# Layer norms of a two-layer decoder trunk: the last column block of the second 128 rows in two half banks, and the modulation after it in program order

## The chip, the cores and the metric

The kernel runs on one core of one Trainium2 chip. The metric is the device time of one execution in microseconds (us). TensorE (PE) multiplies, VectorE (DVE) and ScalarE (ACT) do the elementwise work, GpSimd (POOL) a few tiny operations, and SyncE (SP) issues the loads of the weights. PE writes its products into eight PSUM banks of 512 float32 columns by 128 partitions.

## What is computed

The input is one sequence of 256 rows by 2048 columns in float32. There are two layers, and each has a token mixer (forgetting attention in layer 0, sliding-window attention in layer 1) and a gated feed-forward block. Around each of these four sub-layers stands the same frame:

```python
for i in range(DEPTH):
    h = x * (1.0 + sc1) + sh1
    y = fox_attention(h, ...) if i % 2 == 0 else swa_attention(h, ...)
    x = layer_norm(DEEPNORM_ALPHA * x + (1.0 + g1) * y, ln_mix_g[i], ln_mix_b[i])
    h = x * (1.0 + sc2) + sh2
    y = conv_ffn(h, ...)
    x = layer_norm(DEEPNORM_ALPHA * x + (1.0 + g2) * y, ln_ffn_g[i], ln_ffn_b[i])
```

A layer norm needs the mean and the variance of a whole row of 2048 columns. So the first multiplication of the next sub-layer can't start before the last column of the sub-layer before it is there. There are four such places: three between sub-layers (called the first, second and third boundary here), and the end of the program.

## The kernel before

All products are formed in float32 with a split of both operands: a value is the sum of a rounded high part and a low part, and each product is three matmuls (high by high, high by low, low by high). A weight tile `w` of 256 rows by 512 columns is loaded by SP, ACT rounds it into `wh` (L264), and DVE forms the low part `wl` (L275). `wh` and `wl` have four buffers each, used in turn, so the cast into a buffer waits until PE is through with the tile four places earlier. `stream` (L256) issues all this and keeps a few tiles ahead.

The rows lie in two halves of 128, `t` = 0 and 1. The products that end a sub-layer (the output projection of a mixer in `out_proj`, the down projection in `conv_ffn`) are formed in column blocks of 512 by `x_mm` (L285): for each of the two row halves one bank "xs", three matmuls of 512 columns for each of the K slices. In the last block `x_mm_end` (L294) changes the order: for the last `n` weight tiles (2 in the mixers, 2 and 4 in the two down projections) it does the first row half as the tiles come, keeps the tiles, and does the second row half at the end. So the first half can be evacuated while PE does the second.

`residual` (L620) evacuates a block on DVE, row half by row half: bank times gate (L623), add to `x` (L625), row statistics of these 512 columns (L630). In the last block follow the sums over all blocks (L633), adding epsilon (L635), and the power of minus one half on POOL (L636). For the first row half `nm`, minus mean times reciprocal deviation, is formed too (L629).

`between` (L1103) then leads to the next sub-layer. `normalise` (L640) scales a block of 512 columns in place, the first row half on ACT (L646), the second on DVE (L648). `mod_turn` (L485) transposes a pair of 128-column slices of `x` on PE into banks "sm" (L493), four transposes a pair. `mod_pair` (L497) applies scale and shift and splits the result into `hHL` (high part `hH`, low part `hL`). For the first two pairs it takes the short way: ACT writes `hH` out of the bank (L503), DVE the full value (L504) and `hL` (L505). The later pairs go by L507 on ACT, L508 on DVE, L84 on ACT (which needs both) and L85 on DVE. `modulate` (L515) runs two pairs at once and hangs the other six into a list `feeds`; each following weight tile calls one after its own matmuls. `feed` calls `normalise` for a block of 512 columns whenever its first slice is due.

After the first and third boundary comes the up projection: `u_mm` goes through a weight tile in eight pairs of matmuls, 512 columns of `hHL` (high and low part together) and 256 of `hH`. The tile number n, counted from 1, needs the slices of the pair number n. After the second boundary comes `x_stationary` with `hHL` as the stationary operand.

The order on each engine is made by a scheduler when the program is built, out of the order in which the code records the instructions. `pin` keeps an instruction in the recorded order against others that are pinned; others may be moved. At run time each engine works its list in that fixed order, so an instruction that waits holds up all behind it on its engine.

At the very end the last layer norm is applied on DVE with its weights (L1152, L1153) block by block, and SP issues the eight stores.

## Time and profile before

| | |
|---|---|
| median of three runs | 2256.86 us (2254.90, 2256.86, 2256.91) |
| the profiled execution: its time | 2256.56 us |
| its span on the core | 2254.8 us |
| mean granted TensorE clock | 0.988 |
| instructions | 33096 |
| DVE busy | 1847.4 us |
| ACT busy | 1220.7 us |
| bytes moved | 602.66 MB, 267 GB/s in the mean |

The views used below print one line for an instruction or for a group of them. A line of the timeline has the start and the length in us, the engine, the line of the kernel, the operation, output and input by name, shape and count; in brackets stands how long the engine sat idle before it, and who released it. A line of the windows view has the stretch and its length, then for each engine the time busy and the count, then the granted clock of TensorE (1.00 is full speed), the share of the DMA engines and GB/s. A line of the groups has the total busy time, the mean in ns, and the idle time before. TensorE matmuls are pipelined: the cadence is the distance of two starts, and the printed length of one is longer than that.

### The profile page before, as it was taken

How to read it: one execution, taken by the hardware profiler on the slowest of the kernel's cores; microseconds unless marked ns; L12 is line 12 of the kernel's file. 1: busy time of each engine (PE TensorE's matmuls, PEld its weight loads, DVE VectorE, ACT ScalarE, POOL GpSimd, SP SyncE). 2: the span in 40 equal slices, each digit the busy share in tenths (PEclk: the TensorE clock that was granted, in tenths of full speed). 3: DMA queues.
4: the chain of work that ended last, by engine and by line, in shares of the span. 5: the costliest groups of instructions: out<-in, count | busy, mean ns of one | idle time of the engine just before them, and what ended most of it. 6: DMA issues, size and time to landing. Idle time of an engine off the chain costs nothing. (4 is left out here: it accounts for less than half of the span.)

```text
span 2254.8 us, 33096 instructions
## 1 busy us (share of the span) xinstructions
PE 2196.5 (97%) x12037; PEld 1901.8 (84%) x12037; DVE 1847.4 (82%) x2626; ACT 1220.7 (54%) x2073; POOL 22.6 (1%) x52
## 2 busy tenths in 40 slices
PE   6999999999999999999999999999999999999997
PEld 5999888878888888888887788778888888888886
DVE  6979999979989968799888999769988655676766
ACT  3435656555555543655634588746555533555542
POOL 0000000000000000000000000000000000000000
PEclk9999999999999999999999999999999999999999
DMA  9999999958978989789887777648887555555553
GB/s 336 385 357 345 356 354 325 332 190 302 322 266 296 323 299 336 263 288 317 275 311 283 243 244 244 219 163 263 287 270 257 190 192 195 189 193 188 188 195 112
DMA packets 274228, 602.66 MB, mean 267 GB/s; under 512 B 21062, under 2 KB 29960, under 8 KB 273552
## 3 DMA queue, kind: packets, MB, share of 16 engines
q1 hardware_dynamic: 273008, 595.85, 76.5%
q0 software_dynamic: 1056, 4.69, 0.6%
q8 instruction: 94, 1.54, 0.3%
q14 instruction: 70, 0.57, 0.1%
HBM read 598.37 MB, written 2.10 MB: 266 GB/s over the span
## 5 line engine op out<-in xcount | busy, mean ns | idle before, releaser
L264 ACT CAST wh<-w 128x1024 fp32r<-128x1024 f32 x728 | 763.9, 1051 | 802.5 <-PE us L75 288.4
L275 DVE TENSOR_TENSOR wl<-w,wh 128x1024 fp32r<-128x1024 f32 x728 | 885.9, 1221 | 300.4 <-ACT wh L264 293.7
L75 PE MATMUL us<-hHL,wh 128*128 128x512 f32 x2816 | 985.7, 393 | 3.2 <-DVE hHL L505 3.2
L75 PE MATMUL us<-hHL,wl 128*128 128x256 f32 x2816 | 792.0, 283 | 3.2 <-DVE wl L275 3.2
L75 PEld LDWEIGHTS us<-hHL,wh 128*128 128x128 f32 x2816 | 530.2, 188 | 115.8 <-ACT hHL L503 3.9
L75 PEld LDWEIGHTS us<-hHL,wl 128*128 128x128 f32 x2816 | 534.4, 190 | 8.0 <-DVE wl L275 4.6
L75 PE MATMUL xs<-wh,gT 128*128 128x512 f32 x1408 | 435.7, 390 | 0.0
L75 PEld LDWEIGHTS xs<-wh,gT 128*128 128x128 f32 x1408 | 264.3, 188 | 54.8
L75 PE MATMUL xs<-wl,gT 128*128 128x512 f32 x704 | 273.9, 389 | 0.0
L75 PE MATMUL xs<-wh,hHL 128*128 128x512 f32 x704 | 238.5, 404 | 0.3 <-ACT wh L264 0.2
L404 DVE SCALAR_TENSOR_TENSOR acc<-wa,cact,acc 128x1024 f32<-128x1024 f32 x180 | 228.2, 1276 | 0.0
L75 PE MATMUL ws<-hHL,wh 128*128 128x256 f32 x1024 | 190.1, 288 | 4.4 <-ACT hHL L84 2.1
L75 PEld LDWEIGHTS ws<-hHL,wh 128*128 128x128 f32 x1024 | 162.0, 195 | 7.4 <-ACT hHL L84 2.7
L404 DVE SCALAR_TENSOR_TENSOR acc<-wa,cactp,acc 128x1024 f32<-128x1024 f32 x128 | 162.2, 1277 | 0.0
L75 PEld LDWEIGHTS xs<-wh,hHL 128*128 128x128 f32 x704 | 131.8, 190 | 30.0 <-issue 1.0
L75 PEld LDWEIGHTS xs<-wl,gT 128*128 128x128 f32 x704 | 132.2, 188 | 27.3
L75 PE MATMUL ws<-hHL,wl 128*128 128x256 f32 x512 | 143.7, 288 | 2.2 <-DVE wl L275 2.2
L75 PE MATMUL xs<-wl,hHL 128*128 128x512 f32 x352 | 141.7, 403 | 1.5 <-DVE wl L275 1.4
L75 PE MATMUL xs<-wh,oT 128*128 128x512 f32 x384 | 124.9, 395 | 0.1
L1069 ACT ACTIVATE u<-us,ccol 128x256 f32<-128x256 f32 x176 | 98.1, 562 | 39.4 <-DVE us L1067 39.4
L75 PEld LDWEIGHTS ws<-hHL,wl 128*128 128x128 f32 x512 | 98.4, 195 | 2.9 <-DVE wl L275 2.8
L1070 DVE SCALAR_TENSOR_TENSOR u<-us,ccol,u 128x255 f32<-128x255 f32 x176 | 83.3, 478 | 13.4 <-ACT u L1069 13.3
(217 smaller groups left out, 1753.3 us busy)
## 6 DMA issues: line engine op xcount, KB each, us to landing
w<-in_ffn_w_up_dram SPq DMA_DIRECT2D x352, 512.0 KB, 4.6
wa<-in_ada_w_dram SPq DMA_DIRECT2D x320, 512.0 KB, 5.4
w<-in_ffn_w_down_dram SPq DMA_DIRECT2D x176, 512.0 KB, 3.9
w<-in_fox_w_in_dram SPq DMA_DIRECT2D x96, 512.0 KB, 7.0
wo<-in_ada_w_dram SPq DMA_DIRECT2D x48, 512.0 KB, 9.3
w<-in_swa_w_in_dram SPq DMA_DIRECT2D x40, 512.0 KB, 5.6
w<-in_fox_w_o_dram SPq DMA_DIRECT2D x32, 512.0 KB, 5.5
w<-in_swa_w_o_dram SPq DMA_DIRECT2D x32, 512.0 KB, 5.3
```

The costliest lines, as they stand in the source:

```text
L75: return nc.tensor.matmul(o, lhsT, rhs, start=start, stop=stop, **kw)
L264: pin(nc.scalar.copy(h, w), False)
L275: pin(nc.vector.tensor_tensor(l, w, f32(h), op=ALU.subtract), behind[0] > 0)
L404: pin(nc.vector.scalar_tensor_tensor(ac, wo, (cactp if row else cact)[:, k:k + 1], ac, op0=ALU.mult, op1=ALU.add), True)
L1069: nc.scalar.activation(u, pf, AF.Identity, bias=cw(CW, f), scale=cw(2, f))
L1070: nc.vector.scalar_tensor_tensor(u[:, 1:], pf[:, :S - 1], cw(1, f), u[:, 1:], op0=ALU.mult, op1=ALU.add)
```

## The change

The last block's second row half goes into two banks ("xh") of which 256 columns each are used, instead of one bank of 512. In `x_mm`, each matmul of 512 columns into it becomes two of 256. In `x_mm_end` the kept tiles are gone through once for the first bank and then once for the second. The number of kept tiles goes from 2 to 3 in the mixers and in the first down projection, and stays at 4 in the second. `residual` evacuates each half bank with its own three instructions, and the row statistics of the second row half are taken over 256 columns everywhere (twelve sets: four of 512 columns for the first half, eight of 256 for the second). `nm` stands behind the first half bank.

In `modulate`, blocks 0 and 1 are normalised ahead of the first pair, block 2 with the pair at slice 4, and block 3 with the pair at slice 8. The two instructions of `normalise` and those of the first two pairs on DVE are now pinned. The larger `stats` is paid for in memory: three small tiles of the rotary angles move into one buffer of the temporary pool "t".

```diff
-    def x_banks():
-        return [bank("xs") for _ in range(NT)]
+    def x_banks(halved=False):
+        return [bank("xs") for _ in range(NT - 1)] + [[bank("xh")[:, :256] for _ in range(2)] if halved else bank("xs")]
...
+    def pieces(o):
+        return [(p, slice(n * 256, n * 256 + 256)) for n, p in enumerate(o)] if isinstance(o, list) else [(o, slice(0, WB))]
+
-    def x_mm(ps, kc, h, l, stat, last, first=0, ts=range(NT)):
+    def x_mm(ps, kc, h, l, stat, last, first=0, ts=range(NT), part=slice(0, 2)):
...
-                mm(ps[t], xh, h[:, i, :], start=kc + i == first)
-                mm(ps[t], xh, l[:, i, :])
-                mm(ps[t], xl, h[:, i, :], stop=kc + i == last)
+                for o, c in pieces(ps[t])[part]:
+                    mm(o, xh, h[:, i, c], start=kc + i == first)
+                    mm(o, xh, l[:, i, c])
+                    mm(o, xl, h[:, i, c], stop=kc + i == last)
...
-                for e in kept:
-                    x_mm(ps, *e, stat, nk - 1, ts=(1,))
+                for p in range(len(pieces(ps[1]))):
+                    for e in kept:
+                        x_mm(ps, *e, stat, nk - 1, ts=(1,), part=slice(p, p + 1))
...
-                nc.vector.tensor_scalar(o, ps[j], g, b, op0=ALU.mult, op1=ALU.add)
-                nc.vector.tensor_tensor(hL[:, k + j, :], o, f32(hH[:, k + j, :]), op=ALU.subtract)
+                pin(nc.vector.tensor_scalar(o, ps[j], g, b, op0=ALU.mult, op1=ALU.add), fixed)
+                pin(nc.vector.tensor_tensor(hL[:, k + j, :], o, f32(hH[:, k + j, :]), op=ALU.subtract), fixed)
...
-            if k % 4 == 0:
-                norm(k // 4)
-            mod_pair(G, B, k, mod_turn(k, 2), k < 4)
+            for d in {0: (0, 1), 4: (2,), 8: (3,)}.get(k, ()):
+                norm(d)
+            mod_pair(G, B, k, mod_turn(k, 2), k < 4, False, k < 4)
...
-    stats = cst.tile([P, NT, D // 512, nc.vector.BN_STATS_DIM], F32, name="stats")
+    stats = cst.tile([P, D // 512 + D // 256, nc.vector.BN_STATS_DIM], F32, name="stats")
...
+            for n, (o, c) in enumerate(pieces(ps[t])):
+                cx = slice(d * 512 + c.start, d * 512 + c.stop)
+                xs = x[:, t, cx]
+                nc.vector.tensor_tensor(tmp[:, c], o, gate[:, cx], op=ALU.mult)
+                nc.vector.tensor_tensor(xs, xs, tmp[:, c], op=ALU.add)
+                if last and t == 0:
+                    nc.vector.bn_stats(stats[:, d, :], xs)
+                elif last:
+                    for q in range(cx.start // 256, cx.stop // 256):
+                        nc.vector.bn_stats(stats[:, 4 + q, :], x[:, t, q * 256:(q + 1) * 256])
+                if last and t == 1 and end and n == 0:
+                    mu, rs, nm = moments[0]
+                    pin(nc.vector.scalar_tensor_tensor(nm, mu, -1.0, rs, op0=ALU.mult, op1=ALU.mult))
...
-                nc.scalar.activation(xs, xs, AF.Identity, scale=rs, bias=nm)
+                pin(nc.scalar.activation(xs, xs, AF.Identity, scale=rs, bias=nm))
...
-                nc.vector.tensor_scalar(xs, xs, mu, rs, op0=ALU.subtract, op1=ALU.mult)
+                pin(nc.vector.tensor_scalar(xs, xs, mu, rs, op0=ALU.subtract, op1=ALU.mult))
...
-            use = x_mm_end(ps[d], stat, KC, 2) if d == D // WB - 1 else ...
+            use = x_mm_end(ps[d], stat, KC, 3) if d == D // WB - 1 else ...
...
-                ps = x_stationary(w_dn, ..., (2, 4)[l] if si > 0 and d == D // WB - 1 else 0)
+                ps = x_stationary(w_dn, ..., (3, 4)[l] if si > 0 and d == D // WB - 1 else 0)
```

In the built program each engine's list differs from that of before at these places alone. Three differences of order come from the scheduler and not from the diff. After the first and third boundary, ACT's list has the cast of the sixth weight tile ahead of L84 of the third pair, where before it stood behind it; and DVE's list has L508's counterpart of the fourth pair ahead of L85's of the third. After the second boundary, DVE's list has the third pair's L508 counterpart, which needs transposes that PE does after the first weight tile, ahead of the last `hL` of the second pair and of the low part of the second weight tile. PE's list has the transposes of the fourth, fifth and sixth pairs together ahead of the third weight tile after the first and third boundary.

More of the change, by code (lines that the diff above doesn't have):

```diff
@@ L186, in rotary @@
         inv = [float(np.float32(ROPE_THETA ** (-2.0 * i / ROPE_DIM))) for i in range(HR)]
-        ang = cst.tile([P, NT, HR], F32, name="ang")
+        room = ttile("room").rearrange("p (a t h) -> p a t h", t=NT, h=HR)
+        ang = room[:, 0]
         for i in range(HR):
             nc.vector.tensor_scalar_mul(ang[:, :, i], posc, inv[i])
-        nturn = cst.tile([P, NT, HR], F32, name="nturn")
-        nint = cst.tile([P, NT, HR], I32, name="nint")
+        nturn, nint = room[:, 1], room[:, 2].bitcast(I32)
         nc.vector.tensor_scalar_mul(nturn, ang, 1.0 / (2.0 * math.pi))
@@ L330, in x_stationary @@
     def x_stationary(wsrc, col, k0, nk, stat, end=0):
-        ps = x_banks()
+        ps = x_banks(end > 0)
         use = x_mm_end(ps, stat, nk, end) if end else lambda kc, h, l: x_mm(ps, kc, h, l, stat, nk - 1)
@@ L495, in mod_turn, with mod_pair @@
         return os
-    def mod_pair(G, B, k, ps, fast=False, keep=False):
+    def mod_pair(G, B, k, ps, fast=False, keep=False, fixed=False):
         tmp = ttile()
@@ L622, in residual @@
             tmp = ttile()
-            nc.vector.tensor_tensor(tmp, ps[t], gate[:, d * 512:(d + 1) * 512], op=ALU.mult)
-            xs = x[:, t, d * 512:(d + 1) * 512]
-            nc.vector.tensor_tensor(xs, xs, tmp, op=ALU.add)
-            if last:
-                if t == 1 and d == D // 512 - 1:
+            end = d == D // 512 - 1
+            for n, (o, c) in enumerate(pieces(ps[t])):
[9 more added lines that the diff above has]
+                if last and t == 1 and end and n == 0:
                     mu, rs, nm = moments[0]
                     pin(nc.vector.scalar_tensor_tensor(nm, mu, -1.0, rs, op0=ALU.mult, op1=ALU.mult))
-                nc.vector.bn_stats(stats[:, t, d, :], xs)
-                if d == D // 512 - 1:
-                    mv = sp.tile([P, 2], F32, tag="mv", name="mv")
-                    nc.vector.bn_aggr(mv, stats[:, t].rearrange("p a b -> p (a b)"))
-                    rs = sp.tile([P, 2], F32, tag="rs", name="rs")
-                    nc.vector.tensor_scalar_add(mv[:, 1:2], mv[:, 1:2], EPS)
-                    nc.gpsimd.tensor_tensor(rs[:, 0:1], mv[:, 1:2], mhalf, op=ALU.pow)
-                    moments[t] = (mv[:, 0:1], rs[:, 0:1], rs[:, 1:2])
+            if last and end:
+                mv = sp.tile([P, 2], F32, tag="mv", name="mv")
+                nc.vector.bn_aggr(mv, (stats[:, 4:] if t else stats[:, :4]).rearrange("p a b -> p (a b)"))
+                rs = sp.tile([P, 2], F32, tag="rs", name="rs")
+                nc.vector.tensor_scalar_add(mv[:, 1:2], mv[:, 1:2], EPS)
+                nc.gpsimd.tensor_tensor(rs[:, 0:1], mv[:, 1:2], mhalf, op=ALU.pow)
+                moments[t] = (mv[:, 0:1], rs[:, 0:1], rs[:, 1:2])
             yield
@@ L744, in part @@
         def part(d, ks):
-            use = x_mm_end(ps[d], stat, KC, 2) if d == D // WB - 1 else                 lambda kc, h, l_: x_mm(ps[d], kc, h, l_, stat, KC - 1)
+            use = x_mm_end(ps[d], stat, KC, 3) if d == D // WB - 1 else                 lambda kc, h, l_: x_mm(ps[d], kc, h, l_, stat, KC - 1)
             stream(w_o, 0, d * WB, ks, use)
@@ L757, in out_proj @@
                 then(lambda d=d: ada.update(rate=((1.3, 1.3, 1.3, 1.3), (0.9,) * 4)[l][d]))
-                ps[d] = x_banks()
+                ps[d] = x_banks(d == D // WB - 1)
                 part(d, list(range(KC)))
@@ L1121, in conv_ffn @@
             for d in range(D // WB):
-                ps = x_stationary(w_dn, d * WB, b0 * 4, (b1 - b0) * 4, stat, (2, 4)[l] if si > 0 and d == D // WB - 1 else 0)
+                ps = x_stationary(w_dn, d * WB, b0 * 4, (b1 - b0) * 4, stat, (3, 4)[l] if si > 0 and d == D // WB - 1 else 0)
                 then(lambda ps=ps, d=d, si=si: defer(residual(ps, d, gates[l, 5], si == len(sbs) - 1)),
```

## The prediction

> **What bounds the kernel now.** The page comes first: PE is busy nearly all the time, so the places matter where it isn't.

> ```profile
> PE 2196.5 (97%) x12037; PEld 1901.8 (84%) x12037; DVE 1847.4 (82%) x2626; ACT 1220.7 (54%) x2073; POOL 22.6 (1%) x52
> ```

> Next is PE's timeline at the first boundary.

> ```profile
> 470.24 0.40 PE L75 MATMUL xs<-wh,hHL 128*128 128x512 f32 x1
> 473.07 1.12 PE L493 MATMUL sm<-ident,x 128*128 128x128 f32 x4 [2.43 <-ACT x L646]
> 474.58 1.11 PE L493 MATMUL sm<-ident,x 128*128 128x128 f32 x4 [0.40 <-DVE x L648]
> 477.28 0.77 PE L75 MATMUL us<-hHL,wh 128*128 128x512 f32 x1 [1.58 <-DVE hHL L505]
> ...
> 483.05 0.48 PE L75 MATMUL us<-hHL,wh 128*128 128x512 f32 x1
> ...
> 485.91 0.71 PE L493 MATMUL sm<-ident,x 128*128 128x128 f32 x5
> 486.38 0.48 PE L75 MATMUL us<-hHL,wh 128*128 128x512 f32 x1
> ```

> Call the end of the last matmul (470.64) zero. The next weight tile starts 6.64 us later. It lasts from 477.28 until the transposes ahead of 483.05, over 5 us; the next tile lasts 2.86 (483.05 to 485.91). The windows view says why: the granted clock is halved.

> ```profile
> 322.43:325.84 3.41, 1.96 (x11) 1.49 (x10) 3.25 (x5) 1.04 (x1) 0.00 (x0) 1.00 1.03 377
> 469.21:472.62 3.41, 1.43 (x7) 0.81 (x5) 3.10 (x8) 2.52 (x3) 0.57 (x1) 1.00 0.00 0
> ...
> 479.45:482.86 3.41, 3.41 (x13) 2.92 (x13) 1.86 (x2) 0.26 (x1) 0.00 (x0) 0.50 0.35 137
> ...
> 1230.38:1233.79 3.41, 3.41 (x13) 2.92 (x12) 3.41 (x7) 1.63 (x3) 0.00 (x0) 0.50 0.00 0
> ...
> 1506.86:1510.27 3.41, 3.41 (x13) 2.92 (x13) 1.89 (x2) 0.23 (x1) 0.00 (x0) 0.50 0.42 151
> ```

> The clock changes on a grid of 3.41 us. The stretch with PE busy for 1.43 of it was followed by half clock, that with 1.96 (a pause elsewhere) was not, and full clock came back behind a wholly busy one (482.86, 1233.79, 1510.27). The other two boundaries:

> ```profile
> 1223.41 0.39 PE L75 MATMUL xs<-wh,gT 128*128 128x512 f32 x1
> ...
> 1227.74 1.12 PE L493 MATMUL sm<-ident,x 128*128 128x128 f32 x4 [0.85 <-DVE x L648]
> 1228.87 0.79 PE L75 MATMUL xs<-wh,hHL 128*128 128x512 f32 x1
> ```
> ```profile
> 1497.69 0.40 PE L75 MATMUL xs<-wh,hHL 128*128 128x512 f32 x1
> ...
> 1504.72 0.76 PE L75 MATMUL us<-hHL,wh 128*128 128x512 f32 x1 [1.58 <-DVE hHL L505]
> ```

> There PE is back 5.07 and 6.63 us after zero. The second is shorter because its first four matmuls need no `hL`.

> **What the change moves at a boundary.** DVE's timeline at the first boundary is the path that ends last:

> ```profile
> 470.68 0.69 DVE L623 TENSOR_TENSOR t<-xs,gate 128x512 f32<-128x512 f32 x1 [0.17 <-PE xs L75]
> 471.40 0.69 DVE L625 TENSOR_TENSOR x<-x,t 128x512 f32<-128x512 f32 x1
> ...
> 473.98 1.92 DVE L648 TENSOR_SCALAR x<-x,mv,rs 128x512 f32<-128x512 f32 x4 [0.67 <-POOL rs L636]
> 475.81 0.99 DVE L504 TENSOR_SCALAR t<-sm,G,B 128x256 f32<-128x256 f32 x2
> 476.72 0.75 DVE L505 TENSOR_TENSOR hHL<-t,hHL 128x256 fp32r<-128x256 f32 x2
> ```
> ```profile
> L1067 DVE TENSOR_TENSOR us<-us,c 128x256 f32<-128x256 f32 x176 | 71.1, 424 | 0.0
> ...
> L623 DVE TENSOR_TENSOR t<-xs,gate 128x512 f32<-128x512 f32 x48 | 31.7, 684 | 12.5 <-PE xs L75 12.4
> ```

> 1. *Half the last evacuation.* After zero stand three instructions over 256 columns instead of 512: 3 x (0.684 - 0.424) = 0.78. The sum over 48 statistics instead of 24 costs 0.02 more (by those same two rows, 1 ns an element). L648's place moves from 3.34 to 2.58. The first row half starts 36 matmuls of 256 columns ahead of zero (4.2 us, cadence below) instead of 12 of 512, so it and the first half bank fit in front.

> 2. *Two L648 in front instead of four.* The second transposes start 0.60 behind L648 (474.58), so at 3.18, and ACT takes `hH` out 0.51 behind them (475.09, below): 3.69. DVE is free at 2.58 + 0.46 + 0.54 = 3.58, where before four L648 held it until L504 at 475.81 (5.17). L504 to L505 takes 0.54 + 0.04 and L505 to the first matmul 0.56 (476.72 to 477.28): 3.69 + 0.58 + 0.56 = 4.83. The program order of L504 and L505, singly instead of two and two, is in this.

> So PE is back at 4.83 instead of 6.64 and 6.63: 1.81 and 1.80 gained. At the second boundary the first matmul waits for `hH` (3.69 + 0.56 + 0.15 = 4.40), not for `hL`: 5.07 - 4.40 = 0.67. Together 4.28 us.

> 3. *A wait behind it, at the third weight tile of the first and third boundary.* Before, ACT ran in this order:

> ```profile
> 475.09 1.93 ACT L503 ACTIVATE hHL<-sm,B,G 128x256 fp32r<-128x256 f32 x4 [0.67 <-PE sm L493]
> ...
> 482.60 1.05 ACT L264 CAST wh<-w 128x1024 fp32r<-128x1024 f32 x1 [4.88 <-issue]
> 483.56 0.56 ACT L507 ACTIVATE t<-sm,B,G 128x256 f32<-128x256 f32 x1
> 484.15 0.62 ACT L84 CAST hHL<-t 128x512 fp32r<-128x512 f32 x1
> 485.99 1.05 ACT L264 CAST wh<-w 128x1024 fp32r<-128x1024 f32 x1 [1.22 <-PE us L75]
> ```

> The cast at 485.99 is that of the sixth tile; it waits until PE is through with the second (485.91), and L84 had run. In the new list this cast stands ahead of the third pair's L84, and L85 and PE's third tile wait behind that. From the end of the second tile: 0.08 to the cast, 0.96 to the next of ACT (482.60 to 483.56), L84 0.62, 0.10 to DVE, L85 0.69 (its length as L625's), 0.18 to PE: 2.63. Meanwhile PE does twelve transposes at 0.12 (485.91 to 486.38 for four), 1.41. PE waits 1.2, twice: 2.4 lost. The lower bound is 0 (another order of waits hides it), the upper 2 x 2.6 (the transposes late as well); I take 2.4 as each link has its row.

> 4. *A wait at the second boundary.* DVE's third-pair L508 needs transposes behind the first tile, and the last `hL` and the second tile's `wl` queue behind it: 0.25 + 0.54 + 0.42 + 1.22 (L275) + 0.15 = 2.6 after that tile, while PE has two matmuls and eight transposes, 1.4 at full and 2.8 at half clock. Between 0 and 1.2; I take 0.6.

> ```profile
> L275 DVE TENSOR_TENSOR wl<-w,wh 128x1024 fp32r<-128x1024 f32 x728 | 885.9, 1221 | 300.4 <-ACT wh L264 293.7
> ```

> 5. *Twice as many matmuls.* The four last blocks have 48, 60, 48 and 60 matmuls for the second row half; 216 become 432.

> ```profile
> 265.02 0.40 PE L75 MATMUL ws<-hHL,wh 128*128 128x256 f32 x2
> ...
> 271.67 0.40 PE L75 MATMUL ws<-hHL,wh 128*128 128x256 f32 x2
> ```
> ```profile
> 1217.29 0.62 PE L75 MATMUL xs<-wh,gT 128*128 128x512 f32 x2
> ...
> 1217.97 0.62 PE L75 MATMUL xs<-wh,gT 128*128 128x512 f32 x2
> ```

> 57 matmuls of 256 columns took 6.65 us, 0.117 each; three of 512 took 0.68, 0.227 each. So two halves cost 0.007 more than a whole: 216 x 0.007 = 1.4. With `hHL` in both kinds 512 columns take 0.23, and a half costs exactly half, so the lower bound is 0. I take 0.6.

> 6. *The end of the program.* DVE is the bound there, without a pause but for 0.5 us ahead of L1153:

> ```profile
> 2246.15 1.41 DVE L1152 SCALAR_TENSOR_TENSOR x<-x,mv,ln 128x512 f32<-128x512 f32 x2
> ...
> 2247.47 1.41 DVE L1153 SCALAR_TENSOR_TENSOR x<-x,rs,ln 128x512 f32<-128x512 f32 x2
> ```

> Six instructions of 0.424 for three of 0.684 make it 0.5 longer (0 to 0.8).

> 7. *At nothing.* The halved statistics of the earlier blocks (12 x 0.16 us of DVE) lie under PE's stream, where DVE sat idle 300 us ahead of L275; without that cover they cost 1.9. The third kept tile needs casts 1.4 us apart in front of the last block's end, and they are done up to three tiles early; without that 1 us a boundary. The rotary buffer holds one of four temporaries; the same instructions run, and I know no price but a few tenths.

> 8. *The clock.* Cold work after the restarts was 5.58, 4.92 and 5.55 us (477.28 to 482.86, and so on), and half of it is lost: 8.0. On a grid that lies anywhere against the restart, full clock returns 3.41 to 6.83 us after it, 5.12 in the mean, so 7.7 for three: 0.3 gained, with a spread of about 0.9 on the sum.

> Is the clock cut at all? PE would be idle at 0 to 1.6, 2.2 to 3.2 and 3.8 to 4.8 us, 3.6 of the 4.8, and wherever the grid lies one stretch has PE busy for about 1.5 of 3.41 or less, like the 1.43 that was cut. So yes, mostly. [...]

> **Sum.** 2256.56 (the profiled time, 0.3 under the median) - 4.28 + 2.4 + 0.6 + 0.6 + 0.5 - 0.3 = 2256.1.

> **The rivals.**

> A. As above, the gain given back by new waits: 2256.1, own range 2253.5 to 2258.5. Chance 0.56.

> B. The waits of 3 and 4 do not bind: 2256.1 - 3.0 = 2253.1. For it, all instructions involved are short and ACT has 46% of its time free; against it, both engines work in order and the cast can't run before the second tile ends. 0.19.

> C. The clock is not cut at one or more boundaries: 2.56 gained at each (half of 5.12), 2248.4 for all three. For it, the shortest restart (4.40) leaves stretches of up to 2.0 busy at some positions of the grid, like the 1.96 that was kept; against it, the 1.43. [...] 0.08.

> D. Slower: the third tile's wait cuts the clock a second time. It decides once PE idles between 1.45 us (the kept 1.96 of 3.41) and 1.98 (the cut 1.43) in one stretch, and the wait is put at 1.2. Where it is 0.5 longer, twice, and two cuts cost 2.56 each: 2256.1 + 1.0 + 5.1 = 2262.2. For it, the upper bound 2.6 of step 3; against it, no link of the wait is missing in the rows. 0.14.

> E. Halves do not hide their weight loads, and each matmul lasts as long as a load:

> ```profile
> L75 PEld LDWEIGHTS ws<-hHL,wh 128*128 128x128 f32 x1024 | 162.0, 195 | 7.4 <-ACT hHL L84 2.7 <-ACT wh L264 2.0 <-ACT hHL L503 1.1
> ```

> 216 x (2 x 0.195 - 0.227) = 35: 2291. The cadence of 0.117 with loads of 0.195 in flight speaks against it. 0.03.

> That the change doesn't do what it says is no case: the built order has half banks, two L648 in front and pairs in program order.

> **How the numbers follow.** The likeliest is A, 2256.1. About 0.2% (4.5 us, 2252.3 to 2261.4) is what a measurement can tell from no change. Faster than that: half of B, C, and the low edge of A: 0.24. Slower: most of D, E and the high edge of A: 0.17. Same: 0.59. The range takes in B's 2253.1 with a single uncut boundary (2250.5) and the lower part of D: 2250.5 to 2261.5.

> **What would show it.** Right: PE back 4.8 us after zero at the first and third boundary and 4.4 at the second; in front of the third weight tile a PE wait of about 1.2 on L85, with ACT's cast in front of L84; half clock again at all three; 256-column cadence 0.113 to 0.117; the end 0.5 longer. Wrong: no PE wait in the 15 us after a restart (B), a granted clock of 1.00 throughout a boundary (C), a second stretch of half clock behind the third tile (D), a cadence near 0.19 (E).

## The result and the profile after

| | median | executions |
|---|---|---|
| before | 2256.89 us | 4, 2254.90 to 2258.71 |
| after | 2271.47 us | 4, 2269.83 to 2273.16 |

The change makes the kernel slower: ratio 1.0071, 95% interval 1.0058 to 1.0084, or 14.6 us. The prediction was 2256.1, at most 2261.5. The page of the profiled execution after (span 2271.3 us, mean clock 0.990) shows PE as busy as ever, only for longer:

```profile
PE 2211.4 (97%) x12253; PEld 1915.9 (84%) x12253; DVE 1850.5 (81%) x2650; ACT 1218.9 (54%) x2073; POOL 26.2 (1%) x52
```

PE's busy time grew by 14.9 us (2196.5 to 2211.4). The 216 added matmuls can't explain it by the prediction's step 5 (0.6 us), and the boundaries can't either, since there PE is idle. A stretch far from any boundary gives the answer. The first pair of lines below is the windows view of before and after, restricted to the matmuls of the up projection (`us`), for one stretch of the second feed-forward layer:

```profile
1600.00:1700.00 100.00, 100.00 (x579) 1.00 0.81 266
```
```profile
1600.00:1700.00 100.00, 100.00 (x571) 1.00 0.81 270
```

Both stretches have PE busy all the time at full clock, with the same instructions on the same shapes; after, eight fewer of them fit into 100 us. PE's timeline shows the cadence. First before, then after:

```profile
1619.86 0.39 PE L75 MATMUL us<-hHL,wh 128*128 128x512 f32 x1
1620.09 0.28 PE L75 MATMUL us<-hHL,wl 128*128 128x256 f32 x1
...
1621.94 0.39 PE L75 MATMUL us<-hHL,wh 128*128 128x512 f32 x1
```
```profile
1619.79 0.40 PE L75 MATMUL us<-hHL,wh 128*128 128x512 f32 x1
1620.03 0.28 PE L75 MATMUL us<-hHL,wl 128*128 128x256 f32 x1
...
1621.90 0.40 PE L75 MATMUL us<-hHL,wh 128*128 128x512 f32 x1
```

Six pairs (512 columns with `wh`, then 256 with `wl`) take 2.08 us before and 2.11 after. Over all pairs of the two traces that stand in an unbroken stream, the mean distance from one 512-column start to the next is 346.8 ns before and 351.1 after. There are 2816 pairs, so these 4.3 ns make 12 us. No instruction of the up projection was touched by the diff.

What the diff did touch is memory. `stats` grew from 192 to 288 bytes a partition, and three rotary tiles of 64 bytes left the constants, so everything allocated behind them moved by 96 bytes. In the built programs `hHL` stays at 27904, while the buffers of `wh` move from 119776 to 119680, and those of `w`, `wl` and `gT` by the same 96. From here on "distance" is the first `wh` buffer's address minus that of `hHL`: 91872 before, 91776 after. All buffers of `wh` and `wl` are multiples of 4096 apart.

The boundaries went nearly as forecast. The timeline of after at the first one:

```profile
474.81 0.28 PE L75 MATMUL xh<-wh,hHL 128*128 128x256 f32 x1
...
477.74 1.00 DVE L659 TENSOR_SCALAR x<-x,mv,rs 128x512 f32<-128x512 f32 x2 [0.67 <-POOL rs L647]
478.34 0.65 PE L498 MATMUL sm<-ident,x 128*128 128x128 f32 x4 [1.21 <-DVE x L659]
478.70 1.93 ACT L508 ACTIVATE hHL<-sm,B,G 128x256 fp32r<-128x256 f32 x4 [0.65 <-PE sm L498]
479.30 0.54 DVE L509 TENSOR_SCALAR t<-sm,G,B 128x256 f32<-128x256 f32 x1 [0.56 <-ACT hHL L508]
479.88 0.42 DVE L510 TENSOR_TENSOR hHL<-t,hHL 128x256 fp32r<-128x256 f32 x1
480.45 0.75 PE L75 MATMUL us<-hHL,wh 128*128 128x512 f32 x1 [1.46 <-DVE hHL L510]
...
488.14 1.04 PE L498 MATMUL sm<-ident,x 128*128 128x128 f32 x8
488.27 1.05 ACT L264 CAST wh<-w 128x1024 fp32r<-128x1024 f32 x1 [1.04 <-issue]
489.22 0.61 ACT L84 CAST hHL<-t 128x512 fp32r<-128x512 f32 x1
489.38 0.44 PE L498 MATMUL sm<-ident,x 128*128 128x128 f32 x2 [0.20 <-DVE t L513]
489.87 0.69 DVE L85 TENSOR_TENSOR hHL<-t,hHL 128x512 fp32r<-128x512 f32 x1 [0.54 <-ACT hHL L84]
490.35 0.44 PE L498 MATMUL sm<-ident,x 128*128 128x128 f32 x2 [0.53 <-ACT t L512]
490.61 0.50 PE L75 MATMUL us<-hHL,wh 128*128 128x512 f32 x1
```

Zero is 475.09; PE is back at 5.36 (6.64 before), and the third weight tile waits behind cast, L84 and L85 as the prediction's step 3 had it. At the second boundary PE is back 4.23 us after zero instead of 5.07, with the forecast wait behind it:

```profile
1245.17 0.50 PE L75 MATMUL xs<-wl,hHL 128*128 128x512 f32 x1 [0.76 <-DVE wl L275]
```

### The profile page after: what moved, and what is told of

Same layout as the page of the kernel before. It is cut to its first block, busy times and chain, and to the rows that moved or that the text cites. A ratio compares the mean times of both kernels' runs of the same rounds, so it can differ in the third digit from the quotient of the medians.

```text
span 2271.3 us, 33552 instructions
## 1 busy us (share of the span) xinstructions
PE 2211.4 (97%) x12253; PEld 1915.9 (84%) x12253; DVE 1850.5 (81%) x2650; ACT 1218.9 (54%) x2073; POOL 26.2 (1%) x52
## 3 DMA queue, kind: packets, MB, share of 16 engines
q0 software_dynamic: 1056, 4.69, 0.6%
## 4 chain that ended last, share of the span: by engine, by line
PE 86%; DVE 7%; ACT 3%; DMA 2%; issue 2%; POOL 0%; SPq 0%; DVEq 0%; ACTq 0%; POOLq 0%
PE us L75 43%; PE xs L75 31%; PE ws L75 6%; DVE acc L409 2%; DVE wl L275 2%; PE xh L75 2%; DMA wo<-in_ada_w_dram 1%; PE S L75 1%; ACT wh L264 1%; PE o L75 1%; PE sm L75 1%; PE cps L75 1%; ACT pr L718 0%; PE sm L498 0%; ACT pr L710 0%
## 5 line engine op out<-in xcount | busy, mean ns | idle before, releaser
L264 ACT CAST wh<-w 128x1024 fp32r<-128x1024 f32 x728 | 763.3, 1051 | 819.2 <-PE us L75 297.7
L275 DVE TENSOR_TENSOR wl<-w,wh 128x1024 fp32r<-128x1024 f32 x728 | 887.1, 1223 | 309.5 <-ACT wh L264 301.2
L75 PE MATMUL us<-hHL,wh 128*128 128x512 f32 x2816 | 995.7, 396 | 2.8 <-DVE hHL L510 2.6
L75 PE MATMUL us<-hHL,wl 128*128 128x256 f32 x2816 | 792.8, 283 | 2.7 <-DVE wl L275 2.7
L75 PEld LDWEIGHTS us<-hHL,wh 128*128 128x128 f32 x2816 | 530.0, 188 | 125.8 <-ACT hHL L508 3.2
L75 PEld LDWEIGHTS us<-hHL,wl 128*128 128x128 f32 x2816 | 531.2, 189 | 7.8 <-DVE wl L275 4.0
L75 PE MATMUL xs<-wh,gT 128*128 128x512 f32 x1328 | 413.3, 390 | 0.0
L75 PEld LDWEIGHTS xs<-wh,gT 128*128 128x128 f32 x1328 | 249.3, 188 | 51.3
L75 PE MATMUL xs<-wl,gT 128*128 128x512 f32 x664 | 258.5, 389 | 0.0
L75 PE MATMUL xs<-wh,hHL 128*128 128x512 f32 x688 | 233.6, 404 | 0.4 <-ACT hHL L508 0.3
L75 PE MATMUL ws<-hHL,wh 128*128 128x256 f32 x1024 | 192.8, 290 | 4.4 <-ACT hHL L84 2.1
L75 PEld LDWEIGHTS ws<-hHL,wh 128*128 128x128 f32 x1024 | 163.7, 196 | 6.9 <-ACT hHL L84 2.3
L75 PEld LDWEIGHTS xs<-wh,hHL 128*128 128x128 f32 x688 | 129.3, 190 | 28.7 <-issue 1.0
L75 PE MATMUL ws<-hHL,wl 128*128 128x256 f32 x512 | 145.2, 291 | 2.2 <-DVE wl L275 2.2
L75 PEld LDWEIGHTS xs<-wl,gT 128*128 128x128 f32 x664 | 124.7, 188 | 25.3
L75 PE MATMUL xs<-wl,hHL 128*128 128x512 f32 x344 | 138.3, 403 | 1.8 <-DVE wl L275 1.7
L75 PE MATMUL xs<-wh,oT 128*128 128x512 f32 x336 | 112.0, 396 | 0.1
L75 PEld LDWEIGHTS ws<-hHL,wl 128*128 128x128 f32 x512 | 99.0, 196 | 2.8 <-DVE wl L275 2.6
```

Of the source, the lines that this page charges most:

```text
L75: return nc.tensor.matmul(o, lhsT, rhs, start=start, stop=stop, **kw)
L264: pin(nc.scalar.copy(h, w), False)
L275: pin(nc.vector.tensor_tensor(l, w, f32(h), op=ALU.subtract), behind[0] > 0)
```

## The experiments

Two theories stood at the start. *Place*: the distance between the weight tiles and `hHL` sets the pace of TensorE. *Work*: the halves, the new order or the PSUM banks that follow from them cost it. The figures in brackets behind a ratio are its 95% interval; it is taken against runs of the kernel before on the same chip.

### Memory without the work, and the work without the memory

`e1_after_pad` is the changed kernel with an unused tile beside `posc`:

```diff
+        spare = cst.tile([P, 24], F32, name="spare")
+        nc.gpsimd.memset(spare, 0.0)
```

> The changed kernel with one unused constant tile of 96 bytes a partition added, which puts the weight tiles (w, wh, wl) and gT back at the addresses of the kernel before (wh at 119776 instead of 119680 and so on); hHL was and stays at 27904. Nothing else differs. Place theory (the 96 bytes by which the weight tiles moved against hHL set the pace of the up projection): the pace goes back from about 121.0 ns a 256-column and 231.9 ns a 512-column matmul to about 119.0 and 230.2, which takes some 10 to 12 us off: 2258 to 2262 us. Rival (halves, order of the work and the schedule themselves): the place means nothing, 2270 to 2273 us. Rival (which PSUM banks the up projection's groups take): also 2270 to 2273, as the banks don't move.

`e2_before_moved` is the kernel before with that tile and with the rotary tiles in a temporary buffer:

```diff
-        ang = cst.tile([P, NT, HR], F32, name="ang")
+        spare = cst.tile([P, 24], F32, name="spare")
+        nc.gpsimd.memset(spare, 0.0)
+        room = ttile("room").rearrange("p (a t h) -> p a t h", t=NT, h=HR)
+        ang = room[:, 0]
...
-        nturn = cst.tile([P, NT, HR], F32, name="nturn")
-        nint = cst.tile([P, NT, HR], I32, name="nint")
+        nturn, nint = room[:, 1], room[:, 2].bitcast(I32)
```

> The kernel before with only the memory part of the change: the rotary angle tiles put in a temporary buffer and an unused constant tile of 96 bytes, so that w, wh, wl and gT lie at the addresses of the changed kernel (wh at 119680) and everything ahead of them where it lay. No halves, no new order. Place theory: 121 and 232 ns in the up projection, 2267 to 2269 us. Rival (halves, order, schedule) and rival (banks): 2256 to 2258 us.

Measured: e1 2259.21 us, ratio 1.0012 (1.0002 to 1.0021); e2 2267.97 us, ratio 1.0054 (1.0037 to 1.0071). The same window of the up projection, e1 first, then e2:

```profile
1600.00:1700.00 100.00, 100.00 (x579) 1.00 0.84 269
```
```profile
1600.00:1700.00 100.00, 100.00 (x571) 1.00 0.83 268
```

The count follows the memory and not the work: 579 with all of the change but the old place, 571 with nothing of the change but the new place. The pair's means are 346.8 and 351.1 ns. So the 96 bytes cost 11.2 us alone (2267.97 - 2256.76, before's median in that comparison) and 12.3 within the change (2271.47 - 2259.21). As e1 has the PSUM banks of the changed kernel, these are ruled out too.

`e3_order_alone` has only the new order of normalisation and modulation, `e4_pad_whole` all of e1 but the halves (`x_banks` with `halved = False`).

> The kernel before with only the modulation and the normalisation in program order (two normalisations of the first blocks ahead of the first pairs instead of four); no halves, no memory moved, two kept tiles in the first sub-layer. Place theory: the pace of before (119 and 230 ns); the restarts come 1 to 2 us sooner, the waits at the third weight tile give half of it back: 2253 to 2257 us. Rival (order and schedule cost the pace): 2262 us or more.

> The changed kernel with the 96 unused bytes and with no halves: the last block of the second 128 rows is one bank and one evacuation again, three kept tiles, new order and the finer statistics stay. Place theory: the pace of before; against the padded kernel with halves it saves the 0.012 us that each of 216 pairs of half-width matmuls costs over a whole one (2.6 us) and pays about 0.75 us at each of three boundaries for the longer last evacuation (2.3 us), so within 1.5 us of it: 2256 to 2261 us. Rival (halves are the cause of the loss): 2256 or less, while the padded kernel with halves stays at 2270.

Measured: e3 2258.53 us, 1.0006 (0.9997 to 1.0016), above the 2253 to 2257 expected; e4 2258.70 us, 1.0010 (1.0001 to 1.0019); the pace in both is that of before. Between e1, e3 and e4 the times tell nothing apart; what halves and order do is read from the boundaries further down.

### Which place counts

The kernel before, with the rotary tiles in the temporary buffer and unused tiles of 160 bytes (e5) and 128 (e6) instead of 96; with 32 unused bytes as its only edit (e7); and the changed kernel with its 96 unused bytes ahead of `hHL` (e8):

```diff
-        spare = cst.tile([P, 24], F32, name="spare")
+        spare = cst.tile([P, 40], F32, name="spare")
```
```diff
+    spare = cst.tile([P, 24], F32, name="spare")
+    nc.gpsimd.memset(spare, 0.0)
     hHL = cst.tile([P, KC, 2, S], F32R, name="hHL")
```

> The kernel before with the weight tiles moved by 32 bytes towards hHL (wh at 119744, which is 64 past a multiple of 128 and 0 past a multiple of 64; hHL at 27904, a multiple of 128). Theory 64 (the pace is bad where the weight tiles begin on the same 64-byte phase as hHL): the slow pace, 121 and 232 ns, 2267 to 2269 us. Theory 128 (only the phase 0 of 128 is bad): 119 and 230 ns, 2255 to 2259 us. Theory distance (the farther by any amount from the old place, the slower): a third of the loss, about 2260 us.

> The kernel before with the weight tiles moved by 64 bytes towards hHL (wh at 119712: 32 past a multiple of 64 and of 128). Theory 64 and theory 128: the pace of before, 119 and 230 ns, 2255 to 2259 us. Theory distance: two thirds of the loss, about 2264 us.

> The kernel before with 32 unused bytes behind the constants and nothing else: the weight tiles move by 32 bytes away from hHL (wh at 119808, a multiple of 128). Theory 64 and theory 128: the slow pace, 121 and 232 ns, 2267 to 2269 us, from 32 bytes that nothing reads. Theory distance: not slower by more than a third, or faster (2253 to 2260 us).

> The changed kernel with 96 unused bytes ahead of hHL instead of behind it: hHL moves to 28000 (32 past a multiple of 64) and the weight tiles to the addresses of before (119776, also 32 past a multiple of 64), so that the distance between them is that of the changed kernel. If the distance between weight tile and hHL counts (same 64-byte phase): the slow pace, 121 and 232 ns, 2270 to 2273 us. If the weight tiles' own phase counts: 119 and 230 ns, 2257 to 2261 us.

Measured: e5 2268.02 us, 1.0052 (1.0032 to 1.0072); e6 2266.37, 1.0047 (1.0034 to 1.0060); e7 2264.17, 1.0038 (1.0025 to 1.0052); e8 2271.17, 1.0070 (1.0052 to 1.0089). All four are slower than before. The theories of a 64-byte and a 128-byte phase, which expected the pace of before from e6, fall with it, and that of the mere distance, which expected 2260 from e5, falls with e5. e8 is the one that tells most. Its weight tiles are where before had them, and its pace is that of the changed kernel:

```profile
1600.00:1700.00 100.00, 100.00 (x571) 1.00 0.83 268
```

So it isn't where the weight tiles lie that counts. Nor is it where `hHL` lies, since before and after have it at the same address. What before and after differ in, and after and e8 share, is the distance between the two operands.

### The same phase for both

In every kernel so far the pairs of weight tile and `gT` ran at 227 ns for 512 columns; their distance is 32768. If the phase between the operands counts, the same phase for `hHL` might be best. e9 makes `hHL` ahead of `nsink` and adds 32 bytes; e10 makes `stats` and `mhalf` ahead of `hHL`; e11 is the changed kernel with `hHL` ahead of `nsink` and 128 bytes:

```diff
+    hHL = cst.tile([P, KC, 2, S], F32R, name="hHL")
     nsink = cst.tile([P, SQ], F32, name="nsink")
```

> The kernel before with hHL placed 256 bytes lower (its tile made ahead of three small constants) and 32 unused bytes behind them, so that the weight tiles lie 92160 bytes behind hHL, 45 times 2048: each 512-byte slice that is loaded as weights and each row that is streamed begin on the same phase of 512 and 2048 bytes, as they do where the weight tiles meet gT (32768 bytes apart), the pairs that ran at 227 ns for 512 columns in every kernel so far. Theory phase (the distance modulo 512 or 2048 sets the pace, 0 is best): the up projection goes from 119.0 and 230.2 to about 114 and 227, 340.5 for a pair instead of 349.2, which over 2816 pairs is 24 us, with some 5 us from the mixers: 2226 to 2235 us. Rival (only the old place was good, other distances cost): 2262 to 2270 us. Rival (distance no longer matters within this change): 2256 us.

> The kernel before with the statistics and the constant of the square root (224 bytes together) placed ahead of hHL instead of behind it: hHL moves to 28128, nothing else that TensorE reads moves, and the weight tiles lie 91648 bytes behind it, a multiple of 512 but not of 2048 (1536 over). Theory phase with a period of 512 bytes: as the kernel with the multiple of 2048, 2226 to 2235 us. With a period of 2048: like the others, 2256 to 2270 us.

> The changed kernel with hHL 256 bytes lower and 128 unused bytes behind the small constants, so that the weight tiles lie 92160 bytes behind hHL here too. Theory phase: 14 us less than with the pace of before, plus what the change itself makes at equal pace (within 3 us of nothing by the padded kernels): 2226 to 2238 us, within 3 us of the kernel before at the same distance. If halves and order gain once the pace is equal: 2 to 4 us below it. Rival (place means nothing beyond the old one): 2262 to 2272 us.

Measured: e9 2263.65 us, 1.0034 (1.0020 to 1.0047); e10 2267.92, 1.0047 (1.0030 to 1.0064); e11 2268.01, 1.0054 (1.0039 to 1.0069). The expected gain of 24 us didn't come: equal phase is no rule for the up projection. It does hold for the matmuls that stream the weight tile past `hHL` as weights (`xs<-w,hHL`), whose median start distance was 227 ns in these three and in e7 against 234 before; there are 1056 of them in the kernel before, too few to make up for the rest.

The traces show more. In e7, e9, e10 and e11, whose distances are all multiples of 256 (91904, 92160, 91648, 92160), the pace switches between the same two values. Below is the mean pair, in tenths of ns, of each 128 pairs in order, worked out from the start times in the traces (pairs with a pause between them left out):

```
before            3474 3480 3467 3468 3467 3467 3468 3467 3467 3467 3467 3470 3469 3467 ... 3467
after             3509 3516 3511 3509 3511 3511 3510 3509 3511 3511 3510 3509 3511 3511 ... 3511
e8_all_moved      3511 3512 3512 3509 3511 3511 3510 3508 3511 3511 3510 3510 3511 3511 ... 3511
e7_plus32         3486 3480 3467 3473 3467 3466 3532 3534 3534 3533 3533 3489 3467 3467 ... 3534
e9_same2048       3487 3496 3467 3473 3467 3466 3532 3534 3534 3533 3533 3481 3533 3533 ... 3534
```

e9's two values stand in its windows as well, early in the first feed-forward layer and in the second:

```profile
620.00:700.00 80.00, 78.82 (x443) 1.00 0.82 275
1600.00:1700.00 100.00, 100.00 (x569) 1.00 0.82 261
```

The kernel before has 444 and 579 in these two stretches, the changed one 438 and 571. So at these three distances of 0 modulo 256 the stream ran at the good pace (346.7 ns) or at a worse one (353.3), and stayed there for hundreds of pairs (in e7 and e9 five blocks of 128 in a row at 353.2 to 353.4). e7 and e9 change at the same places in the first layer; what makes the stream change isn't shown.

### The other three phases

> The kernel before with the weight tiles 128 bytes nearer to hHL (distance 91744, 96 modulo 256; before has 224). Period of 128: the pace of before to the nanosecond, 118 and 228 in most, 2255 to 2259 us. Period of 256 with one good place: 352 to 354 ns for a pair, 2264 to 2268 us. Period of 256 with several good places: anything from 2250 to 2268 us.

> The kernel before with the weight tiles 160 bytes nearer to hHL (distance 91712, 64 modulo 256). Period of 128: as the place 32 bytes nearer (119.8 and 233.0 ns, 2268 us). Period of 256 with one good place: 352 to 354 ns for a pair, 2264 to 2268 us. Several good places: down to 2250 us.

> The kernel before with the weight tiles 192 bytes nearer to hHL and no unused bytes at all (distance 91680, 32 modulo 256); it is what taking the rotary tiles out of the constants alone would have made. Period of 128: as the place 64 bytes nearer (118.5 and 233.5 ns, 2266 us). Period of 256 with one good place: 352 to 354 ns for a pair, 2264 to 2268 us. Several good places: down to 2250 us.

They are e2 with unused tiles of 64, 32 and 0 bytes. Measured: e12 2257.06 us, 1.0005 (0.9995 to 1.0014); e13 2270.68, 1.0063 (1.0048 to 1.0078); e14 2269.97, 1.0054 (1.0035 to 1.0073). The windows of e12 and e13:

```profile
1600.00:1700.00 100.00, 100.00 (x578) 1.00 0.82 267
```
```profile
1600.00:1700.00 100.00, 100.00 (x567) 1.00 0.82 268
```

All eight phases that steps of 32 bytes can reach:

| distance modulo 256 | kernels | pair in steady stretches, ns | time, us |
|---|---|---|---|
| 224 | before, e1, e3, e4 | 346.7 | 2255.8 to 2259.2 |
| 96 | e12 | 346.7 | 2257.1 |
| 192 | e5 | 348.9 or 353.3 | 2268.0 |
| 160 | e6 | 350.0 | 2266.4 |
| 128 | after, e2, e8 | 351.1 | 2268.0 to 2271.5 |
| 32 | e14 | 346.7 or 353.3 | 2270.0 |
| 0 | e7, e9, e10, e11 | 346.7 or 353.3 | 2263.7 to 2268.0 |
| 64 | e13 | 353.3 | 2270.7 |

Two of the eight are good throughout, and before had one of them. A period of 128 doesn't hold: 64 and 192 differ, and so do 0 and 128. With a period of 256 every run fits: 91648, 91904 and 92160 show the same two values. That is the one phase tried at more than one distance; for the other seven the period is an assumption. No place was found that beats before's.

### Halves and order at equal pace

What the rest of the change is worth was read at the boundaries: the time from zero to PE's restart, and from zero to the start of the 97th matmul of the up projection, at the first and third boundary. The 97th matmul also depends on how long the clock stayed halved behind the restart, which differs from one execution to the next: e12, whose instructions at the boundaries are those of before, had 4.01 and 4.57 us of it where before had 5.58 and 5.55. In that time, at a granted clock of 0.50, the pairs of before came 0.64 us apart (478.05, 478.69, 479.33) instead of 0.347, so 0.46 of the work in it, close to half, is lost. The last column therefore takes half of it off, and there e12 and before agree to 0.1 us.

| | restart, first / third | 97th matmul | half clock before it | 97th matmul less half of that |
|---|---|---|---|---|
| before | 6.64 / 6.63 | 28.51 / 28.50 | 5.58 / 5.55 | 25.72 / 25.72 |
| e12, memory alone | 6.64 / 6.63 | 27.81 / 28.06 | 4.01 / 4.57 | 25.80 / 25.78 |
| e3, order alone | 6.20 / 6.26 | 28.49 / 28.45 | 3.74 / 3.54 | 26.61 / 26.68 |
| e1, order and halves | 5.36 / 5.42 | 28.33 / 27.56 | 5.22 / 3.41 | 25.72 / 25.85 |

The order comes 0.4 earlier at the restart, but 0.9 later at the 97th matmul at equal clock, so 1.3 is lost in between. The halves gain 0.84 at the restart and keep it. Together they stand where before stands. e15 and e16 test whether the wait at the third tile takes the gain: the third pair goes straight from PSUM, like the first two, in e1 and in e3. e17 is e16 with that edit at the first and third boundary alone.

```diff
-            mod_pair(G, B, k, mod_turn(k, 2), k < 4, False, k < 4)
+            mod_pair(G, B, k, mod_turn(k, 2), k < 6, False, k < 4)
```

> The padded changed kernel (weight tiles at the old addresses, halves, new order) with the third pair of blocks (k = 4) modulated like the first two, ScalarE straight from PSUM into hH, so that no cast of the modulated rows stands behind a weight cast. If the wait at the third weight tile is what gives the gain back: no gap of 0.2 and 0.5 us ahead of the third tile, the 64th matmul behind the first and third restart at about 12.4 us instead of 13.0 to 13.9, about 1 to 2 us less in all: 2256.5 to 2258.5 us against 2259. If the halves and the order cost it elsewhere: no change, 2258.5 to 2260 us. If the extra 0.7 us of VectorE work per boundary binds instead: 2260 to 2262 us.

> The kernel with the new order alone (no halves, memory as before) and the third pair modulated like the first two. If the wait at the third tile gave the order's gain back: 0.4 us at each of two restarts and the waits saved, 2255 to 2257.5 us against 2258.5 with the wait. Otherwise 2258 to 2260 us.

> The kernel with the new order alone, the third pair modulated like the first two at the first and third boundary only (ahead of the feed-forward layers) and as before at the second. If the boundaries add up: 400 matmuls behind the second restart at 86.4 us again instead of 87.7, 73.4 and 69.7 us at the others, some 1.2 us less than the last run: 2255 to 2256.5 us, 0.05 to 0.15% under before. If such gains are lost in the spread from run to run: not told apart from before, 2256 to 2258 us.

e15's timeline at the first boundary, between the second and the third tile:

```profile
486.39 1.04 PE L500 MATMUL sm<-ident,x 128*128 128x128 f32 x8
...
486.52 1.05 ACT L266 CAST wh<-w 128x1024 fp32r<-128x1024 f32 x1 [0.57 <-ACT x L659]
487.19 0.48 PE L75 MATMUL us<-hHL,wh 128*128 128x512 f32 x1
```

The same cast runs, but the third tile no longer waits for it. It starts 0.80 us behind the first of the transposes ahead of it (eight of them), where in the changed kernel it was 2.47 (twelve, and 0.73 of waiting). The 97th matmul comes at 26.42 and 26.45 in e15, and at 27.21 and 27.30 in e16. Less half of their half clock (3.26 to 3.41 us) that is 24.71 and 24.78, and 25.58 and 25.61: 1.0 to 1.1 earlier than in e1 and e3. At the second boundary the edit costs 0.7 to 0.9: the 401st matmul behind it starts 98.42 us after zero in e16, and 96.99 and 97.75 in e3 and e17, which don't have it there; with half of the half clock taken off (3.79, 2.79 and 3.79) it is 96.52, 95.59 and 95.85.

The times: e15 2258.00 us, 1.0001 (0.9992 to 1.0010); e16 2256.55, 0.9997 (0.9987 to 1.0006); e17 2255.91, 0.9996 (0.9987 to 1.0005). The gain at the first and third boundary is shown; that any of these kernels is faster than before is not.

What the halves cost is in e1's timeline ahead of the second boundary:

```profile
1221.97 0.28 PE L75 MATMUL xh<-wl,gT 128*128 128x256 f32 x1
...
1223.77 0.28 PE L75 MATMUL xh<-wl,gT 128*128 128x256 f32 x1
```

15 matmuls of 256 columns in 1.80 us are 0.120 each, so two take 0.239 to 0.240 (their mean over the last blocks is 119.3 to 119.6 ns with `gT` and `oT`), against 0.227 for a whole one.

## Why the prediction was wrong, step by step

**The step that failed is step 7**, "at nothing". It weighed the rotary buffer by its instructions ("the same instructions run, and I know no price but a few tenths") and didn't price the move of 96 bytes that came with it and with the larger `stats`. That move cost 11.2 us by itself and 12.3 inside the change, five sixths of the 14.6. The sum had no term for it, as every term stood at a boundary or in the added work. Without it (e1, 2259.21) the time lies inside the stated range.

Step 1 held: L659 (L648 before) starts 2.65 after zero, forecast 2.58.

Step 2 forecast too large a gain, by one link. PE was to be back at 4.83 and came at 5.36; ACT's L508 starts at 3.61 (forecast 3.69), but DVE's L509 waits 0.56 for it, where the sum had DVE start beside it. Restarts gained 1.28, 0.84 and 1.21 in e1, 3.33 instead of 4.28. The second boundary was nearly right (4.23, forecast 4.40).

Step 3 held in its mechanism and its price: cast, L84, L85, third tile, in that order, so rival B is out. The view shows only 0.20 and 0.53 of PE idle, as transposes fill the rest, but taking the wait out moved the 97th matmul by 1.0 to 1.1 us at equal clock (e1 to e15, e3 to e16), forecast 1.2. The transposes were priced a little high: the row that was read as four has five, 0.11 us apart, so twelve take 1.3 and not 1.41.

Step 4 forecast a wait of 0.6; it was 0.76. More is lost behind that restart than this wait: at equal clock e1 starts its 401st matmul 0.3 to 0.5 behind e12 and before (95.11 us after zero against 94.81 and 94.63), though it restarted 0.84 earlier. What the rest is stays open.

Step 5 was mis-sized, and its upper bound too: 0.012 us a pair instead of 0.003, 216 x 0.012 = 2.6 us instead of 0.6 (at most 1.4). The bounds came from 256-column matmuls with `hHL` in the mixers and from half of a whole matmul; most of the new halves have `gT` or `oT`.

Step 6 put 0.5 on the end, at least 0 and at most 0.8; nothing came of it. The last matmul of the program, before and after:

```profile
2241.09 0.39 PE L75 MATMUL xs<-wh,gT 128*128 128x512 f32 x1
```
```profile
2257.71 0.28 PE L75 MATMUL xh<-wh,gT 128*128 128x256 f32 x1
```

From its end to the end of the span it took 13.3 us in both (spans 2254.8 and 2271.3). From the last aggregate of the statistics it is 9.0 before and 9.6 after, but this aggregate comes as much earlier behind the last matmul.

Step 8 was right that the clock is cut at all three boundaries, so rival C is out. The windows view of after on the grid of the clock, at the three boundaries (the granted clock is the third number from the end):

```profile
477.05:480.46 3.41, 0.74 (x6) 0.46 (x5) 2.14 (x6) 2.77 (x6) 0.55 (x1) 1.00 0.01 2
480.46:483.87 3.41, 3.41 (x11) 2.93 (x12) 3.31 (x7) 0.87 (x2) 0.00 (x0) 0.50 0.02 5
...
1234.81:1238.22 3.41, 1.53 (x9) 1.06 (x10) 2.11 (x6) 2.75 (x5) 0.55 (x1) 1.00 0.02 8
1238.22:1241.64 3.42, 3.42 (x10) 2.65 (x10) 2.95 (x7) 2.36 (x5) 0.00 (x0) 0.50 0.00 0
1507.88:1511.29 3.41, 0.76 (x6) 0.43 (x5) 2.42 (x7) 3.05 (x4) 0.55 (x1) 1.00 0.00 0
1511.29:1514.70 3.41, 2.26 (x7) 1.75 (x8) 2.63 (x6) 2.63 (x5) 0.00 (x0) 0.50 0.00 0
```

A stretch with PE busy for 1.53 of 3.41 was followed by half clock, beside the 1.43 of before. The third tile brought no second cut (rival D), and the halves run at 0.12, not at the 0.19 of their loads (rival E). The size of step 8 was off: the half clock behind the restarts lasted 3.41, 3.41 and 4.58 us in this execution, 11.4 together where before had 16.05, and that is 2.3 us less lost, not 0.3. It isn't the change that does this, since e12, with the boundaries of before, had 12.3. In the 57 boundaries of the nineteen traces it lasted 2.07 to 6.16 us, 4.04 in the mean, where the step had 3.41 to 6.83 and 5.12. One reason shows in e9 at the second boundary: full clock came back behind a stretch in which PE was busy for only 3.20.

```profile
1229.61:1233.02 3.41, 3.20 (x10) 2.33 (x11) 3.41 (x9) 2.68 (x6) 0.00 (x0) 0.50 0.00 0
1233.02:1236.44 3.42, 3.42 (x22) 2.95 (x22) 3.42 (x6) 1.71 (x3) 0.00 (x0) 1.00 0.00 0
```

At equal pace and equal clock, the change without its 96 bytes comes to this against before: 0.0 and 0.1 us at the first and third boundary (the last column of the table above), 0.3 to 0.5 at the second, 2.6 for the halves, nothing at the end. That is 3.0 to 3.2 us slower, where the prediction's sum was 0.5 faster; e1 measured 2.4 slower, with an interval of 0.5 to 4.7. So even without the 96 bytes the change would not have gained. What the halves gain at the restarts (0.84, 0.69 and 0.84 between e3 and e1) is paid for by their 2.6, and what the order gains by the waits behind it.

## What to carry to other kernels

A change that resizes, adds or drops a tile also moves every tile allocated behind it, and the place of TensorE's two operands against each other was worth 11.2 us here (e2), more than the 4.28 that the change was to gain at the restarts: look at the built addresses of both, and hold them where they were with an unused tile before a comparison is read. When a kernel gets slower everywhere by a per cent, count the instructions of one shape in an undisturbed stretch of both traces before looking at the places that were edited. A halved matmul should be priced from rows with the same operands. And places in two traces behind a pause can be compared only with the time at half clock (2.07 to 6.16 us here) read off beside them.

## What the runs showed of the hardware

e2 and e8 show that the place sets the pace, by 1.2% here (346.8 to 351.1 ns a pair). Why it does, no run here shows.
